# Hybrid encoder block, down-projection: the gating of the last two blocks of columns stands in the sixth product

## The chip, the cores and the metric

The kernel runs on one core of one Trainium2 chip. The metric is the device time of one execution in microseconds (us); several executions are timed and their median is given. Engines: PE multiplies matrices (TensorE), DVE, ACT and POOL work on vectors, SP issues the DMAs.

## What is computed

One layer of a streaming encoder on x of 2048 frames x 1024 columns in fp32. Only the end of the second sub-layer matters here:

```python
val, gte = jnp.split(u, 2, axis=-1)
x = x + (1 + gate2[:, None, :]) * ((val * jax.nn.silu(gte)) @ w_down[l])
return rms_norm(x, g_final)
```

The hidden matrix `val * silu(gte)` is 2048 x 2816, `w_down` is 2816 x 1024. `x` on the right is the residual after the first sub-layer, called x2 in the kernel.

## The kernel before

**Products.** The up- and the down-projection are multiplied by a scheme of Strassen's kind: each operand is cut into 2 x 2 blocks, and seven products of sums of blocks take the place of eight products. The down-projection (lines 1526 to 1683) runs the seven as a loop over p = 0 to 6; the text calls p = 5 the sixth product and p = 6 the seventh. A product is 1024 frames by 512 columns, summed over 1408 hidden columns, so 11 slices q of 128. The frames are eight tiles tt of 128. Each fp32 value is split into a high and a low part (`pinned_parts`, line 1405), and PE does three matmuls per slice and tile: high by high, high by low, low by high; 24 per slice, 264 per product.

**Order on PE.** The slices of a product go in groups, (0,1,2), (3,4), (5,6), (7), (8,9,10). Within a group PE takes the tiles in the order 0, 2, 3, 4, 1, 5, 6, 7, and for each the slices of the group (line 1675). A tile's result is read out of PSUM (`evict`) right behind its last slice in the last group. The results of tiles 0 and 1 lie in one PSUM tile `v`, the others have a tile `d` each.

**Loads and preparations.** `load_down` (1395) issues three DMAs from SP for a slice: two halves of the hidden columns (`hid_s`) into `ring`, a pool of 10 buffers, and the weight (`wd_s` or `w_down`) into a tile `h`. `prep_down` (1410) makes their parts: ACT copies the high parts (line 1406), POOL subtracts for the low part of the weight, DVE for the low parts of the two halves, `wua` (tiles 0 to 3) and `wub` (tiles 4 to 7) (line 1407). `next_down` (1423) prepares one slice. Ahead of a group of slices starting at g, slices up to g + 5 are prepared (PD = 6), so the sixth product's loop prepares its slices 3 to 10 and the seventh's 0 to 2.

**Order on the other engines.** `pin` keeps every instruction of this part in the order of the code on its engine. Work on results is spread among the preparations: `evict` puts generators into `todo`, and `do_later` (line 1637) takes a number of steps of them after each preparation (DL = 5, so the five steps of one tile). Steps of POOL that need a sum of squares from ACT follow one preparation later (`behind_y`).

**The end of the block.** After the sixth product, u holds what the blocks share, v the fourth product. The generator `c22` of a tile makes v = u + v, y = v x gt2 (the gate), y = y + x2 on POOL, u = u x gt2, x21 = x21 + u. `norm_y` lets ACT sum the squares of y and POOL multiply y by the gain. The seventh product is then added to x21, which gives the other half of the row; `finish` scales both by the root and stores them. `gt2` already holds the gate for both halves of the columns. `load_x2` (1556) loads the residual in four DMAs of 512 KB into the tiles h_5 (x22) and h_6 (x21); before, it is called for the last two blocks at the last group of the sixth product.

Of the kernel before, what the change touches and what calls it, by code (L numbers as in the profile page):

```python
# [8 lines left out]
F = mybir.dt.float32  # L9
# [3 lines left out]
ALU = mybir.AluOpType  # L13
# [3 lines left out]
P = 128  # L17
# [3 lines left out]
CH = 512  # L21
# [26 lines left out]
def hybrid_block(ctx, tc, x, c, w_ada, b_ada, g1, w_in, w_fg2, b_fg2, g_gla, w_out, g2,  # L48
                 w_up, w_conv, b_conv, w_down, g_fin, out):
    nc = tc.nc  # L50
    act, dve, pool, pe, dma = nc.scalar, nc.vector, nc.gpsimd, nc.tensor, nc.sync
# [8 lines left out]
    def sb(stack, name, bufs, side=None):  # L60
        return stack.enter_context(tc.tile_pool(name=name, bufs=bufs, side=side, reuse_waits="tile"))
# [1034 lines left out]
    sums = early_sums()  # L1096
    with in_order(("PE",)):
        for n in range(last_step):
# [16 lines left out]
            v = n - LEAD  # L1115
# [3 lines left out]
            if 0 <= v < N:  # L1119
                value(v)  # L1120
                u, s = divmod(v, 4)
# [34 lines left out]
    DL = 5  # L1156
# [284 lines left out]
    for n in range(2 * NF):  # L1441
        half, f = divmod(n, NF)
# [11 lines left out]
        if n == MW[0] - 2:  # L1454
            gt2 = eone.tile([P, D], F, name="gt2")
# [70 lines left out]
    with est as st:  # L1526
        yp = sb(st, "yp", 1)
        smalle = sb(st, "smalle", 4)
        gfin = yp.tile([P, D], F, name="gfin")
# [26 lines left out]
        def load_x2(i, blk, n):  # L1556
            tiles, ts = eight(i)
            for k, t_ in enumerate(ts):
                pin(dma.dma_start(out=t_, in_=x2_s[k // 2 * 2 + blk][k % 2 * 2 * P:(k % 2 + 1) * 2 * P, n * CH:(n + 1) * CH]
                                  .rearrange("(a p) n -> p a n", p=P)))  # L1560
            return tiles

        def tt_(eng, o, a, b, op):
            pin(eng.tensor_tensor(out=o, in0=a, in1=b, op=op))  # L1564

        nsl = [slice(n * CH, (n + 1) * CH) for n in range(2)]
        u, v = eight(3)[0], eight(4)[0]
        ys, sums, late, todo, behind_y = {}, {}, [], [], []

        def square(tt, y, tag):  # L1570

            ss = smalle.tile([P, 1], F, name=tag)
            junk = raw(None)
            pin(act.activation(out=junk, in_=y, func=AF.Square, scale=D ** -0.5, accum_out=ss))
            return ss

        def first_y(tt, n, x2):

            y = ys[tt]
            tt_(pool, y, y, x2, ALU.add)  # L1580

            def norm_y():
                sums[tt] = square(tt, y, f"ss{tt}")
                tt_(pool, y, y, gfin[:, nsl[n]], ALU.mult)
            behind_y.append(norm_y)
            yield

        def second_y(blk, n, tt, y):
            late.append(finish(blk, n, tt, y, square(tt, y, "ss"), ys[tt], sums[tt]))
            next(late[-1])  # L1590
            for g_ in late[-1 - LC:-LC]:
                next(g_)

        def mid():
            if late:
                next(late[-1])

        def evict(p, tt, ps):
            if p == 0:
                pin(act.activation(out=u[tt], in_=ps, func=AF.Copy))  # L1600
            elif p == 1:
                ys[tt] = yp.tile([P, CH], F, name=f"y{tt}")
                tt_(dve, ys[tt], ps, gt2[:, nsl[0]], ALU.mult)
                todo.append(first_y(tt, 0, x2[tt]))
            elif p == 2:
                tt_(dve, u[tt], ps, u[tt], ALU.add)
            elif p == 3:
                pin(act.activation(out=v[tt], in_=ps, func=AF.Copy))
            elif p == 4:
                y = raw(None)  # L1610
                tt_(dve, y, ps, u[tt], ALU.add)
                mid()
                tt_(dve, y, y, gt2[:, nsl[1]], ALU.mult)
                tt_(dve, y, y, x2[tt], ALU.add)
                second_y(0, 1, tt, y)
            elif p == 5:
                tt_(dve, u[tt], ps, u[tt], ALU.add)

                def c22(tt=tt, x22=x2[tt], x21=x2_last[tt]):
                    ys[tt] = yp.tile([P, CH], F, name=f"y{tt}")  # L1620
                    tt_(dve, v[tt], u[tt], v[tt], ALU.add)
                    yield
                    tt_(dve, ys[tt], v[tt], gt2[:, nsl[1]], ALU.mult)
                    yield
                    yield from first_y(tt, 1, x22)
                    tt_(dve, u[tt], u[tt], gt2[:, nsl[0]], ALU.mult)
                    yield
                    tt_(dve, x21, x21, u[tt], ALU.add)
                    yield
                todo.append(c22())  # L1630
            else:
                y = raw(None)
                tt_(dve, y, ps, x2_last[tt], ALU.add)
                mid()
                second_y(1, 0, tt, y)

        def do_later(n):

            for f_ in behind_y:
                f_()  # L1640
            behind_y.clear()
            for _ in range(n):
                while todo and next(todo[0], True):
                    todo.pop(0)

        acc = {}
        for p in range(7):
            begin = p not in (1, 4)
            for g in groups:
                while done < min(p * NQ2 + g[0] + PD, 7 * NQ2):  # L1650
                    next_down()
                    done += 1
                    if g[-1] != NQ2 - 1 or p < 6:
                        do_later(DL)
                last = g[-1] == NQ2 - 1
                if last and p in (4, 6):
                    do_later(len(todo) * 8)
                    do_later(0)
                if last and p in (1, 4, 5):
                    x2 = load_x2(5, p // 5, int(p != 1))  # L1660
                    if p == 5:
                        x2_last = load_x2(6, 1, 0)
                for tt in (0, 2, 3, 4, 1, 5, 6, 7):
                    if g[0] == 0 and begin:
                        if tt < 2:
                            t_ = pds[0].tile([P, HT], F, name="v") if tt == 0 else t_
                            acc[tt] = t_[:, tt * CH:(tt + 1) * CH]
                        else:
                            acc[tt] = pds[1].tile([P, CH], F, name=f"d{tt}")
                    ps = acc[tt]  # L1670
                    tsl = slice(tt % 4 * P, (tt % 4 + 1) * P)
                    for q in g:
                        hd, w = hids[p, q, tt // 4], w_d[p, q]
                        for m, (l_, r_) in enumerate(((0, 0), (0, 1), (1, 0))):
                            pin(pe.matmul(out=ps, lhsT=hd[:, l_, tsl], rhs=w[:, r_], start=begin and q == 0 and m == 0,  # L1675
                                          stop=q == NQ2 - 1 and m == 2, skip_group_check=not begin))
                    if last:
                        evict(p, tt, ps)
            if p in (4, 6):
                next(late[-1])  # L1680
                for g_ in late[-LC:]:
                    next(g_)
                late.clear()
# [25 lines left out]
```

## Time and profile before

| | |
|---|---|
| three executions | 2638.04, 2641.04, 2641.20 us |
| median | 2641.04 us |
| the profiled execution | 2639.18 us |
| its span, first to last instruction | 2637.5 us |
| PE busy | 2516.4 us, 95% |
| DVE, ACT, POOL busy | 1734.3, 1326.7, 1259.3 us |
| mean granted clock of PE | 0.988 of full |

The time of an execution holds 1.7 us around the span of its instructions. All times in the rows below count from the start of the span. Busy shares are of the whole program; the down-projection is the last 437 us of it. A timeline row gives the start, the duration, the engine, the line, the operation and its operands without buffer numbers (`x1` to `x27` is how many instructions the row merges), and, in brackets, how long the engine was idle before and what released it. POOL's rows for the end of the block have line 1564, that of the helper `tt_`; the tile names tell them apart: `h` tiles hold u, v, x2 and the parts of weights, `y` the first half of a row, `gt` the gate, and the residual's DRAM name reads `x_s`.

### The profile page before, as it was taken

To read this page: it belongs to the slowest core of one execution; us is meant where nothing else is said; L and a number is where in the kernel's file an instruction comes from. 1 tells how busy PE (TensorE), PEld (TensorE's weight loads), DVE (VectorE), ACT (ScalarE), POOL (GpSimd) and SP (SyncE) were. 2 spreads that over 40 slices of the span, in tenths; PEclk is the share of its full clock that TensorE was granted. 3 is DMA by queue.
4 is the path that set the end of the run, shared out by engine and by line. 5 is a ranking of instruction groups with operands and counts; after the bars stand their busy time and mean duration, and the time that the engine had idled before them with its cause. 6 is when DMAs were issued, how large, how long until landed. Compare 5 with 4: busy or idle time off the path is not lost. (4 is left out here: it accounts for less than half of the span.)

```text
span 2637.5 us, 36661 instructions
## 1 busy us (share of the span) xinstructions
PE 2516.4 (95%) x12118; PEld 2063.4 (78%) x12118; DVE 1734.3 (66%) x2332; ACT 1326.7 (50%) x2416; POOL 1259.3 (48%) x1074
## 2 busy tenths in 40 slices
PE   5899999999899999999989999989999999999998
PEld 5788778888678777777768888868888887888886
DVE  6525642144887999999668777776555556454668
ACT  4523234232776888888544444455455544333343
POOL 2202121121654656777346655677676663262336
PEclk9999999999999999999989999999999999999999
DMA  8657953576875544555555555576566557544472
GB/s 287 186 168 239 304 190 118 178 221 178 240 237 164 141 131 144 162 171 156 179 184 187 186 183 180 184 247 224 178 209 216 184 187 244 186 144 128 156 273 98
DMA packets 420558, 499.47 MB, mean 189 GB/s; under 512 B 38270, under 2 KB 262796, under 8 KB 418320
## 3 DMA queue, kind: packets, MB, share of 16 engines
q1 hardware_dynamic: 420368, 497.12, 59.1%
q8 instruction: 96, 1.57, 0.3%
q14 instruction: 94, 0.77, 0.1%
HBM read 330.81 MB, written 166.20 MB: 188 GB/s over the span
## 5 line engine op out<-in xcount | busy, mean ns | idle before, releaser
L1009 POOL TENSOR_TENSOR bt<-bt,om 128x512 f32<-128x512 f32 (+2 forms) x320 | 314.7, 988 | 219.5 <-DVE om L1007 121.5
L1186 POOL TENSOR_TENSOR wub<-ring,wub 128x512 fp32r<-128x512 f32 x172 | 239.5, 1404 | 180.7 <-ACT wub L1185 178.8
L1257 PE MATMUL v<-h,wub 128*128 128x512 f32 x1056 | 251.9, 395 | 14.1 <-DVE v L1261 14.1
L1257 PE MATMUL v<-h,wua 128*128 128x512 f32 x1056 | 259.6, 395 | 4.0 <-DVE eh L912 4.0
L1257 PE MATMUL g<-h,wub 128*128 128x512 f32 x1056 | 255.8, 391 | 2.9 <-DVE g L1261 2.9
L1007 DVE TENSOR_TENSOR_SCAN om<-sg,om,zero 128x513 f32<-128x513 f32 x189 | 240.5, 1273 | 16.0 <-ACT sg L1001 14.6
L1257 PEld LDWEIGHTS v<-h,wub 128*128 128x128 f32 x1056 | 200.7, 191 | 59.4 <-DVE v L1261 9.8
L1257 PEld LDWEIGHTS v<-h,wua 128*128 128x128 f32 x1056 | 199.8, 189 | 49.4 <-ACT wub L1185 4.2
L1257 PEld LDWEIGHTS g<-h,wub 128*128 128x128 f32 x1056 | 199.3, 189 | 45.4 <-DVE g L1261 3.3
L1186 POOL TENSOR_TENSOR wua<-ring,wua 128x512 fp32r<-128x512 f32 x129 | 179.4, 1399 | 115.9 <-ACT wua L1185 111.2
L1675 PE MATMUL d<-h,wub 128*128 128x512 f32 x924 | 222.9, 391 | 0.0
L1407 POOL TENSOR_TENSOR h<-h,h 128x512 fp32r<-128x512 f32 x77 | 114.0, 1483 | 213.1 <-ACT h L1406 190.0
L70 PE MATMUL tr<-ident,bt 128*128 128x128 f32 x1120 | 180.1, 277 | 35.6 <-DVE al L131 24.1
L131 DVE TENSOR_TENSOR al<-tr,ah 128x512 fp32r<-128x512 f32 (+1 forms) x320 | 193.0, 603 | 19.4 <-ACT ah L130 18.8
L1675 PEld LDWEIGHTS d<-h,wub 128*128 128x128 f32 x924 | 173.5, 188 | 37.6
L287 POOL TENSOR_TENSOR wr<-wst,wr 128x1024 fp32r<-128x1024 f32 x28 | 69.7, 2496 | 278.0 <-ACT wr L286 278.0
L130 ACT ACTIVATE ah<-tr 128x512 fp32r<-128x512 f32 (+1 forms) x320 | 179.7, 562 | 25.4 <-PE tr L70 25.1
L70 PEld LDWEIGHTS tr<-ident,bt 128*128 128x128 f32 x1120 | 126.7, 140 | 82.9 <-DVE al L131 34.8
L1334 DVE SCALAR_TENSOR_TENSOR cval<-v,conv_w,cval 128x1023 f32<-128x1023 f32 x44 | 56.4, 1282 | 182.5 <-ACT cval L1326 172.7
L1002 ACT ACTIVATE bt<-z 128x512 f32<-128x512 f32 (+2 forms) x320 | 173.7, 543 | 0.0
L401 PE MATMUL mm<-wr,hh 128*128 128x512 f32 (+1 forms) x448 | 169.7, 379 | 3.6 <-DVE vt L131 2.1
L403 PE MATMUL mm<-wr,hl 128*128 128x512 f32 (+1 forms) x448 | 167.8, 375 | 0.0
(312 smaller groups left out, 6010.2 us busy)
## 6 DMA issues: line engine op xcount, KB each, us to landing
ring<-in_w_up_dram SPq DMA_DIRECT2D x154, 256.0 KB, 3.8
ring<-hid_s SPq DMA_DIRECT2D x154, 256.0 KB, 4.2
wst<-in_w_in_dram SPq DMA_DIRECT2D x45, 512.0 KB, 7.6
wu_s<-ring SPq DMA_DIRECT2D x88, 256.0 KB, 2.4
hid_s<-cval SPq DMA_DIRECT2D x88, 256.0 KB, 2.3
ring<-wu_s SPq DMA_DIRECT2D x88, 256.0 KB, 4.7
kt<-k_hl SPq DMA_DIRECT2D x80, 256.0 KB, 3.3
vt<-v_hl SPq DMA_DIRECT2D x80, 256.0 KB, 3.2
```

Of the source, the lines that this page charges most:

```text
L70: pe.transpose(out=o, in_=i, identity=ident)
L130: act.activation(out=hi, in_=ps, func=AF.Copy)
L131: dve.tensor_tensor(out=lo, in0=ps, in1=f32(hi), op=ALU.subtract)
L401: pe.matmul(out=ps[:, :n], lhsT=hh[:, k, sl], rhs=wh, start=k == 0, stop=False)
L403: pe.matmul(out=ps[:, :n], lhsT=hl[:, k, sl], rhs=wh, start=False, stop=k == KD - 1)
L1002: act.activation(out=b1, in_=z[:, :w], func=AF.Sigmoid, scale=0.125)
L1007: dve.tensor_tensor_scan(out=om[:, 0:n_][:, ::-1], data0=beta[:, 0:n_][:, ::-1], data1=zero[0][:, 0:1].broadcast_to([P, n_]), initial=firs ...
L1009: pool.tensor_tensor(out=b1, in0=b1, in1=om[:, 1:w + 1], op=ALU.mult)
L1186: eng.tensor_tensor(out=t_[:, 1], in0=src, in1=f32(t_[:, 0]), op=ALU.subtract)
L1257: pe.matmul(out=ps, lhsT=lhsT, rhs=rhs, start=begin and k == 0 and m == 0, stop=k == KH - 1 and m == 2, skip_group_check=not begin)
L1407: pin(eng.tensor_tensor(out=t_[:, 1], in0=src, in1=f32(t_[:, 0]), op=ALU.subtract))
L1675: pin(pe.matmul(out=ps, lhsT=hd[:, l_, tsl], rhs=w[:, r_], start=begin and q == 0 and m == 0, stop=q == NQ2 - 1 and m == 2, skip_group_che ...
```

## The change

The work of `c22` is divided in two. A new generator `ahead_of_last` does what needs no sixth product: v = u + v, u = u x gt2, v = v x gt2, x21 = x21 + u, v = v + x22 (POOL). It is put into `todo` for all tiles at the start of the sixth product, so its steps stand among that product's preparations, and `load_x2` for the last two blocks is called at the start of the sixth product as well. The eviction of the sixth product writes the result twice, multiplied by each half of the gate, into y and u; `last_sums` then makes y = y + v on POOL and x21 = x21 + u on DVE, two steps per tile, among the seventh product's preparations.

```diff
--- before.py
+++ after.py
@@ -1614,25 +1614,39 @@
                 tt_(dve, y, y, x2[tt], ALU.add)
                 second_y(0, 1, tt, y)
             elif p == 5:
-                tt_(dve, u[tt], ps, u[tt], ALU.add)
-
-                def c22(tt=tt, x22=x2[tt], x21=x2_last[tt]):
-                    ys[tt] = yp.tile([P, CH], F, name=f"y{tt}")
-                    tt_(dve, v[tt], u[tt], v[tt], ALU.add)
-                    yield
-                    tt_(dve, ys[tt], v[tt], gt2[:, nsl[1]], ALU.mult)
-                    yield
-                    yield from first_y(tt, 1, x22)
-                    tt_(dve, u[tt], u[tt], gt2[:, nsl[0]], ALU.mult)
+                ys[tt] = yp.tile([P, CH], F, name=f"y{tt}")
+                tt_(dve, ys[tt], ps, gt2[:, nsl[1]], ALU.mult)
+                tt_(dve, u[tt], ps, gt2[:, nsl[0]], ALU.mult)
+
+                def last_sums(tt=tt, x21=x2_last[tt]):
+                    tt_(pool, ys[tt], ys[tt], v[tt], ALU.add)
+
+                    def norm_y():
+                        sums[tt] = square(tt, ys[tt], f"ss{tt}")
+                        tt_(pool, ys[tt], ys[tt], gfin[:, nsl[1]], ALU.mult)
+                    behind_y.append(norm_y)
                     yield
                     tt_(dve, x21, x21, u[tt], ALU.add)
                     yield
-                todo.append(c22())
+                todo.append(last_sums())
             else:
                 y = raw(None)
                 tt_(dve, y, ps, x2_last[tt], ALU.add)
                 mid()
                 second_y(1, 0, tt, y)
+
+        def ahead_of_last(tt, x22, x21):
+
+            tt_(dve, v[tt], u[tt], v[tt], ALU.add)
+            yield
+            tt_(dve, u[tt], u[tt], gt2[:, nsl[0]], ALU.mult)
+            yield
+            tt_(dve, v[tt], v[tt], gt2[:, nsl[1]], ALU.mult)
+            yield
+            tt_(dve, x21, x21, u[tt], ALU.add)
+            yield
+            tt_(pool, v[tt], v[tt], x22, ALU.add)
+            yield
 
         def do_later(n):
 
@@ -1646,20 +1660,21 @@
         acc = {}
         for p in range(7):
             begin = p not in (1, 4)
+            if p == 5:
+                x2, x2_last = load_x2(5, 1, 1), load_x2(6, 1, 0)
+                todo.extend(ahead_of_last(tt, x2[tt], x2_last[tt]) for tt in (0, 2, 3, 4, 1, 5, 6, 7))
             for g in groups:
                 while done < min(p * NQ2 + g[0] + PD, 7 * NQ2):
                     next_down()
                     done += 1
                     if g[-1] != NQ2 - 1 or p < 6:
-                        do_later(DL)
+                        do_later(DL if p < 6 else 2)
                 last = g[-1] == NQ2 - 1
-                if last and p in (4, 6):
+                if last and p in (4, 5, 6):
                     do_later(len(todo) * 8)
                     do_later(0)
-                if last and p in (1, 4, 5):
-                    x2 = load_x2(5, p // 5, int(p != 1))
-                    if p == 5:
-                        x2_last = load_x2(6, 1, 0)
+                if last and p in (1, 4):
+                    x2 = load_x2(5, 0, int(p != 1))
                 for tt in (0, 2, 3, 4, 1, 5, 6, 7):
                     if g[0] == 0 and begin:
                         if tt < 2:
```

DVE, the beginning of the sixth product. Before, the preparations of its slices 3, 4 and 5 follow each other (`wua`, `wub`: the two halves; `ring`: the loaded halves):

```order
L1407 TENSOR_TENSOR wua4_23734<-ring_23471,wua4_23734 128x512
L1407 TENSOR_TENSOR wub0_23737<-ring_23472,wub0_23737 128x512
L1407 TENSOR_TENSOR wua5_23749<-ring_23510,wua5_23749 128x512
L1407 TENSOR_TENSOR wub1_23752<-ring_23511,wub1_23752 128x512
L1407 TENSOR_TENSOR wua0_23764<-ring_23725,wua0_23764 128x512
L1407 TENSOR_TENSOR wub2_23767<-ring_23726,wub2_23767 128x512
```

and with the change (`h2_3` holds u, `h2_4` v, `h2_6` the residual x21, `gt2` the gate):

```order
L1407 TENSOR_TENSOR wua4_23750<-ring_23471,wua4_23750 128x512
L1407 TENSOR_TENSOR wub0_23753<-ring_23472,wub0_23753 128x512
L1564 TENSOR_TENSOR h2_4_0_21339<-h2_3_0_21335,h2_4_0_21339 128x512
L1564 TENSOR_TENSOR h2_3_0_21335<-h2_3_0_21335,gt2_16878 128x512
L1564 TENSOR_TENSOR h2_4_0_21339<-h2_4_0_21339,gt2_16878 128x512
L1564 TENSOR_TENSOR h2_6_0_23733<-h2_6_0_23733,h2_3_0_21335 128x512
L1407 TENSOR_TENSOR wua5_23770<-ring_23510,wua5_23770 128x512
L1407 TENSOR_TENSOR wub1_23773<-ring_23511,wub1_23773 128x512
L1564 TENSOR_TENSOR h2_4_1_21340<-h2_3_1_21336,h2_4_1_21340 128x512
```

Four operations of one tile stand behind each preparation, eight times in all.

DVE, the passage from the sixth to the seventh product. Before, each tile is evicted by one operation (`d7` is the last one's result), and between two preparations stand four operations of one tile:

```order
L1564 TENSOR_TENSOR h2_3_3_21338<-d6_23829,h2_3_3_21338 128x512
L1564 TENSOR_TENSOR h2_3_3_21338<-d7_23839,h2_3_3_21338 128x512
L1407 TENSOR_TENSOR wua3_24194<-ring_24035,wua3_24194 128x512
L1407 TENSOR_TENSOR wub5_24197<-ring_24036,wub5_24197 128x512
L1564 TENSOR_TENSOR h2_4_0_21339<-h2_3_0_21335,h2_4_0_21339 128x512
L1564 TENSOR_TENSOR y0_24200<-h2_4_0_21339,gt2_16878 128x512
L1564 TENSOR_TENSOR h2_3_0_21335<-h2_3_0_21335,gt2_16878 128x512
L1564 TENSOR_TENSOR h2_6_0_24097<-h2_6_0_24097,h2_3_0_21335 128x512
L1407 TENSOR_TENSOR wua4_24215<-ring_24074,wua4_24215 128x512
L1407 TENSOR_TENSOR wub0_24218<-ring_24075,wub0_24218 128x512
```

With the change each tile is evicted by two, and one operation stands between two preparations:

```order
L1564 TENSOR_TENSOR h2_3_2_21337<-d5_23850,gt2_16878 128x512
L1564 TENSOR_TENSOR y6_24226<-d6_23860,gt2_16878 128x512
L1564 TENSOR_TENSOR h2_3_3_21338<-d6_23860,gt2_16878 128x512
L1564 TENSOR_TENSOR y7_24238<-d7_23870,gt2_16878 128x512
L1564 TENSOR_TENSOR h2_3_3_21338<-d7_23870,gt2_16878 128x512
L1407 TENSOR_TENSOR wua3_24250<-ring_24091,wua3_24250 128x512
L1407 TENSOR_TENSOR wub5_24253<-ring_24092,wub5_24253 128x512
L1564 TENSOR_TENSOR h2_6_0_23733<-h2_6_0_23733,h2_3_0_21335 128x512
L1407 TENSOR_TENSOR wua4_24267<-ring_24130,wua4_24267 128x512
L1407 TENSOR_TENSOR wub0_24270<-ring_24131,wub0_24270 128x512
L1564 TENSOR_TENSOR h2_6_1_23734<-h2_6_1_23734,h2_3_1_21336 128x512
```

SP. Before, the eight loads of the residual (`x2_s`) stand behind the loads of the seventh product's slice 4 (`h2_0_2_24078`):

```order
L1399 DMA ring_24075<-hid_s1_2_121 128x512
L1402 DMA h2_0_2_24078<-wd_s3_129 128x512
L1559 DMA h2_5_0_24089<-x2_s1_101 128x2x512
L1559 DMA h2_5_1_24090<-x2_s1_101 128x2x512
L1559 DMA h2_5_2_24091<-x2_s3_103 128x2x512
L1559 DMA h2_5_3_24092<-x2_s3_103 128x2x512
L1559 DMA h2_6_0_24097<-x2_s1_101 128x2x512
L1559 DMA h2_6_1_24098<-x2_s1_101 128x2x512
L1559 DMA h2_6_2_24099<-x2_s3_103 128x2x512
L1559 DMA h2_6_3_24100<-x2_s3_103 128x2x512
L1399 DMA ring_24185<-hid_s0_2_114 128x512
L1399 DMA ring_24186<-hid_s1_2_121 128x512
```

With the change they stand right behind the last store of the fifth product's results, ahead of the loads of the sixth product's slice 5 (`h2_0_0_23745`):

```order
L1548 DMA out_0_dram<-ring_23698 128x512
L1559 DMA h2_5_0_23725<-x2_s1_101 128x2x512
L1559 DMA h2_5_1_23726<-x2_s1_101 128x2x512
L1559 DMA h2_5_2_23727<-x2_s3_103 128x2x512
L1559 DMA h2_5_3_23728<-x2_s3_103 128x2x512
L1559 DMA h2_6_0_23733<-x2_s1_101 128x2x512
L1559 DMA h2_6_1_23734<-x2_s1_101 128x2x512
L1559 DMA h2_6_2_23735<-x2_s3_103 128x2x512
L1559 DMA h2_6_3_23736<-x2_s3_103 128x2x512
L1399 DMA ring_23741<-hid_s0_5_117 128x512
L1399 DMA ring_23742<-hid_s1_5_124 128x512
L1402 DMA h2_0_0_23745<-wd_s2_128 128x512
```

Eleven slices' loads are passed. On POOL, `ahead_of_last` puts one sum behind each of the first eight preparations of the sixth product; its operations in the seventh stay three per tile. On PE and ACT the order stays.

## Rows read from the trace of the kernel before

**Rows 1.** Page, part 1: busy us (share of the span) and instructions.
```profile
PE 2516.4 (95%) x12118; PEld 2063.4 (78%) x12118; DVE 1734.3 (66%) x2332; ACT 1326.7 (50%) x2416; POOL 1259.3 (48%) x1074
```

**Rows 2.** Chain of waits, end of the program: start us, us, what.
```profile
2609.99 1.69 POOL h L1407
...
2613.05 7.07 PE d L1675 x27
```

**Rows 3.** Timeline, PE: start us, us, engine, line, operation, output<-inputs, count, [idle time before <-what ended it].
```profile
2502.47 2.20 PE L1675 MATMUL v<-h,wua 128*128 128x512 f32 x9
...
2518.87 1.52 PE L1675 MATMUL v<-h,wua 128*128 128x512 f32 x6
...
2546.20 2.20 PE L1675 MATMUL v<-h,wua 128*128 128x512 f32 x9
...
2562.60 2.20 PE L1675 MATMUL v<-h,wua 128*128 128x512 f32 x9
...
2606.34 1.75 PE L1675 MATMUL v<-h,wua 128*128 128x512 f32 x7
...
2611.71 1.34 PE L1675 MATMUL v<-h,wua 128*128 128x512 f32 x2 [3.63 <-POOL h L1407]
...
2621.99 6.34 PE L1675 MATMUL d<-h,wub 128*128 128x512 f32 x27
```

**Rows 4.** Windows: busy us of PE, PEld, DVE, ACT, POOL (instructions), clock, DMA share, GB/s.
```profile
2612.00:2614.00 2.00, 2.00 (x5) 1.46 (x6) 2.00 (x3) 0.00 (x0) 1.34 (x1) 0.50 0.00 0
2614.00:2616.00 2.00, 2.00 (x8) 1.59 (x8) 1.93 (x4) 0.00 (x0) 0.71 (x1) 0.78 0.00 0
```

**Rows 5.** Timeline, DVE, seventh product, a turn of one frame tile.
```profile
2565.33 0.69 DVE L1564 TENSOR_TENSOR y<-h,gt 128x512 f32<-128x512 f32 x1
...
2566.66 1.67 DVE L1564 TENSOR_TENSOR h<-h,h 128x512 f32<-128x512 f32 x1
...
2568.25 1.79 DVE L1407 TENSOR_TENSOR wua<-ring,wua 128x512 fp32r<-128x512 f32 x1
...
2572.38 0.69 DVE L1564 TENSOR_TENSOR y<-h,gt 128x512 f32<-128x512 f32 x1
```

**Rows 6.** Timeline, POOL, the same turn.
```profile
2566.10 1.68 POOL L1564 TENSOR_TENSOR y<-y,h 128x512 f32<-128x512 f32 x1 [17.18 <-DVE y L1564]
2567.74 1.75 POOL L1407 TENSOR_TENSOR h<-h,h 128x512 fp32r<-128x512 f32 x1
```

**Rows 7.** Windows, sixth product, where the loads run; columns as in rows 4.
```profile
2528.00:2531.00 3.00, 3.00 (x15) 2.48 (x14) 3.00 (x4) 2.03 (x5) 1.83 (x2) 1.00 1.05 388
```

**Rows 8.** Timeline, SP: the loads of slice 6.5 and the x2 loads.
```profile
2513.41 1.32 SPq L1399 DMA_DIRECT2D ring<-hid_s  x2
...
2514.85 0.44 SPq L1402 DMA_DIRECT2D h<-wd_s  x1
...
2535.41 5.83 SPq L1559 DMA_DIRECT2D h<-x_s  x8
```

**Rows 9.** Timeline, ACT: first copy of slice 6.5.
```profile
2518.36 0.63 ACT L1406 ACTIVATE h<-h 128x512 fp32r<-128x512 f32 x1 [3.53 <-DMA h<-wd_s]
```

**Rows 10.** Instructions on the tile x_s, 2534 to 2542: landing of the x2 loads.
```profile
DMA to landing us min/median/max: 6.7/9.1/11.4
```

**Rows 11.** Timeline, DVE, sixth product: subtractions, and the first eviction.
```profile
2512.78 1.37 DVE L1407 TENSOR_TENSOR wua<-ring,wua 128x512 fp32r<-128x512 f32 x1 [1.05 <-ACT wua L1406]
...
2520.84 0.68 DVE L1407 TENSOR_TENSOR wub<-ring,wub 128x512 fp32r<-128x512 f32 x1
...
2548.44 0.69 DVE L1564 TENSOR_TENSOR h<-v,h 128x512 f32<-128x512 f32 x1 [0.68 <-PE v L1675]
```

**Rows 12.** Line 131 (duration ns min/median/max); the page, part 5.
```profile
L131 DVE TENSOR_TENSOR al<-tr,ah x320: 387/662/692, 672.0 to 1289.2; 128x512 fp32r<-128x512 f32 x128, 128x256 fp32r<-128x256 f32 x32
...
L1009 POOL TENSOR_TENSOR bt<-bt,om 128x512 f32<-128x512 f32 (+2 forms) x320 | 314.7, 988 | 219.5 <-DVE om L1007 121.5
```

## Prediction

> **Names.** The seven products of the down-projection are counted from one, the eleven slices of each from zero: slice 6.4 is slice 4 of the sixth product (index 5 in the code). The *preparation* of a slice is three copies on ACT, one subtraction on POOL (weight) and two on DVE (the two halves of the hidden columns, first wua, then wub). A slice is 24 matmuls for the eight frame tiles.
>
> **What bounds the kernel now.** I read the page first: PE is busy for 95% of the span [rows 1], so time can only come from stretches where PE waits. The chain of waits shows one in the part that the change touches: just before the end it leaves PE and runs through POOL's subtraction for a weight [rows 2]. The PE timeline gives its price. The sixth product runs from 2502.47 to 2562.60, which is 60.13 us or 0.228 us for each of 264 matmuls. The seventh would end at 2562.60 + 60.13 = 2622.73, and ends at 2621.99 + 6.34 = 2628.33: 5.60 us are lost [rows 3]. Of these 3.63 are the idle time before slice 7.10's low weight part; the other 1.97 pass right behind it, where the granted clock is 0.50 and then 0.78, between the 1.2 and 2.4 GHz levels [rows 4].
>
> Why is that weight late? In the seventh product DVE needs 7.05 us for one tile's turn (2565.33 to 2572.38) [rows 5], against 24 x 0.228 = 5.47 us that PE spends on a slice. The turn holds six DVE and three POOL operations, and their rows show that they go one at a time: POOL's sum ends at 2567.78, and DVE's addition, begun at 2566.66, ends at 2568.33, 0.55 later; POOL's next ends 1.16 after that, DVE's next 0.55 later again [rows 5, 6]. So a turn is six times about 0.6 plus three times about 1.15.
>
> **The change, by counts.** Per frame tile, four DVE operations leave the seventh product and one comes back; four DVE and one new POOL operation go into the sixth product's preparations; the sixth eviction has two DVE operations in place of one. In all 16 DVE and 8 POOL operations are added. The eight x2 loads move on SP from behind the load of slice 7.4 to before that of slice 6.5.
>
> *What goes.* With three DVE and three POOL operations, a turn of the seventh product takes 3 x 0.6 + 3 x 1.15 = 5.25 us, under PE's 5.47. The 5.60 us can go: **-5.6**.
>
> *The loads.* Eight x2 tiles of 0.524 MB stand in front of a stretch of SP's loads in which the queue moved 388 GB/s at a DMA share of 1.05 [rows 7]: 1.35 us a tile, 10.8 us for all. Before, slice 6.5's three loads (0.786 MB, 2.03 us at that rate) went out from 2513.41 [rows 8] and ACT could start on them at 2518.36 [rows 9], 4.95 us later, so 2.9 us come on top of the transfer. The first tile that DVE adds to is the fifth load: 5 x 1.35 + 2.9 = 9.65 us, so 2523.1. The loads of before took 6.7 to 11.4 us to land [rows 10]; that spread, 2520 to 2525, bounds it. The trace's rate can be weighed against a rule: the Trainium skill (Perfetto Trace Analysis, Roofline) says that a core working alone can draw about 435 GB/s from its 16 DMA engines. The trace shows 388 where the engines are full. By the page's figure the eight tiles would take an estimated 9.6 us, and the sum below would be 1.2 us smaller.
>
> *DVE behind them.* DVE works in order. Tile 0's fourth operation (the addition to x2) waits until 2523.1, and behind it stands the preparation of slice 6.4, which before was done at once behind 6.3's (first of these at 2512.78 [rows 11]). Now its first half ends at 2523.1 + 2 x 0.65 = 2524.4. PE wants it for the sixth matmul of the group that starts at 2518.87 [rows 3], at 2520.0. PE idles **4.4 us**, and if this costs clock as the idle time of 3.63 did, 2 more. POOL's new sum waits less long, for the first x2 tile.
>
> *DVE as the bound.* Slice 6.5 lands 10.8 later, at 2529.2. Its last DVE operation ended 3.16 us behind its landing before (2520.84 + 0.68 [rows 11], less 2518.36): 2532.3. From there each preparation carries one tile's four operations: six DVE and two POOL operations, the turn of rows 5 without one POOL operation, 7.05 - 1.15 = 5.9 us. No row shows this mix. It lies between 4.1 (six at 0.69, nothing held up) and 7.05; I take 5.9 because the rows nearest to it have the same operations in the same turn. It is more than PE's 5.47, so DVE never catches up. Slice 6.10 is five turns on, at 2561.8, its first half 0.6 before: 2561.2. PE wants it seven matmuls into the last group, 2546.20 + 1.6 = 2547.8 [rows 3]. That is 13.4 us late, more than the 6.4 that PE has lost by itself, so 13.4 holds and the first wait is inside it. The rest of the product, 16.4 - 1.6 = 14.8 us, brings PE to 2576.0, or 2578 at a lower clock.
>
> *The evictions.* DVE's sixth turn ends at 2567.7. Two bare preparations (7.1, 7.2; two DVE and one POOL operation, 2.4 us each) come next: 2572.5. Only then do the evictions run. Before they cost nothing, one 0.69 us operation per tile at PE's pace [rows 11]. Now the seventh product's first matmul needs the bank pair of tiles 0 and 1 free, and tile 1 is the fifth evicted: ten operations of 0.65, 2579.0. Their inputs come from PSUM; an operation of that kind never took over 0.692 us in 320 instances, in a stage that had POOL at work on 314.7 us of sums [rows 12], so I count no hold-up. PE is ready before that, so the seventh product starts at 2579.0, not 2562.60: **+16.4**.
>
> **Sum:** 16.4 - 5.6 = **+10.8 us**. The profiled execution took 2639.18 us, so 2650.0. The median of the runs before is 2641.04, 1.9 above it; the prediction is for a median: **2651.8**. The stretch behind the last matmul (9.2 us to the end of the span) stays. ACT's copies stay as many, and in their order.
>
> **Rivals.**
> *Only the first wait (12%).* If DVE's and POOL's operations hold each other up less in this mix, a turn stays under 5.47, DVE catches up within the sixth product, and the change trades one wait for another: 4.4 + 2.0 - 5.6 = +0.8, 2641.8. For it: in the same stretch of before, some DVE subtractions took 0.68 [rows 11]. Against: those are the ones with no POOL operation under way.
>
> *Faster (6%).* The new POOL and DVE work fits into the sixth product, where both have idle time now. This needs the fifth x2 tile by about 2518.7, so that slice 6.4 is ready at 2520.0, and a turn under 5.47. Then only the gain is left: -5.6, 2635.4. Against it: a landing under 5.3 us, where the shortest seen is 6.7 [rows 10], and eight tiles need 10.8 in all.
>
> *The seventh product falls behind as well (12%).* Slice 7.10 is due 2606.34 - 2562.60 + 1.6 = 45.3 us after the product's start [rows 3], at 2624.3. DVE ends its 16 evictions at 2572.5 + 16 x 0.65 = 2582.9 and has eight turns to go: at 5.25 us, 2624.9. That is on the edge; a head start of POOL during the evictions decides for me. With 6.0 a turn it would be 2630.9: 6.6 late and 2 for the clock, +19.4, 2660.4.
>
> That the change doesn't do what it says is excluded by the order of instructions, where the work stands in the sixth product on DVE, POOL and SP.
>
> **Numbers.** My forecast has 70%. A measurement of this kernel can tell about 0.2%, 5.3 us, from no change. The forecast and the third rival are slower by more: 82%. The first rival is the same: 12%. The second is faster, just past the bound: 6%. Range: with a turn of 7.05, six turns add 6.9, with 2 for the clock +19.7, 2660.7, which also takes in the third rival; I end at 2661. Downwards the forecast with a turn of 5.5 is 2.4 less, with the x2 tiles 1.5 early 3.9 less; half way from there to the first rival is about 2643, where I stop. Left out are the faster case and most of the first rival.
>
> **What the profile would show.** Right: DVE idle until about 2523 for an x2 load; PE idle 4 us near 2520 for wua; a second, longer gap near 2556 in the sixth product's last group; evictions from about 2572, as a row without gaps; the seventh product's first matmul near 2579, with PE waiting for DVE; no gap after it, last matmul near 2639. Wrong: evictions that begin near 2548 at PE's pace (first rival), no gap at 2520 (second), a gap behind 2615 (third). Turns of DVE in the sixth product of less than 5.5 us would break the step on which most rests.

## The result, and the profile after

The changed kernel takes **2658.94 us** (median of 4 runs, 2650.61 to 2661.38) against 2640.14 for the kernel before (4 runs, 2638.04 to 2641.2). The ratio is 1.0069, with a 95% interval of 1.0057 to 1.0082: slower by 18.8 us, where the prediction had 10.8 and a range up to 2661.

Every number below is from the profiled execution of each kernel. The changed kernel's has a span of 2659.6 us and a time of 2661.38, the longest of its four. Page, part 1: busy us (share of the span) and instructions.

```profile
PE 2526.8 (95%) x12118; PEld 2069.1 (78%) x12118; DVE 1749.5 (66%) x2348; ACT 1327.6 (50%) x2416; POOL 1271.0 (48%) x1082
```

Beside [rows 1] this shows the 16 added DVE and 8 added POOL operations and the same 12118 matmuls. PE is busy 10.4 us longer with them, though it has no more to do: some ran at a lower clock. The PE timeline shows where (start us, us, engine, line, operation, output<-inputs, count, [idle time before <-what ended it]).

```profile
2505.15 2.20 PE L1690 MATMUL v<-h,wua 128*128 128x512 f32 x9
...
2524.03 0.50 PE L1690 MATMUL v<-h,wua 128*128 128x512 f32 x1 [1.41 <-POOL h L1407]
2528.97 0.79 PE L1690 MATMUL v<-h,wua 128*128 128x512 f32 x1 [4.44 <-DVE wua L1407]
...
2559.98 0.96 PE L1690 MATMUL v<-h,wua 128*128 128x512 f32 x3 [1.07 <-POOL h L1407]
2565.86 1.22 PE L1690 MATMUL v<-h,wua 128*128 128x512 f32 x2 [4.92 <-POOL h L1407]
...
2579.18 4.21 PE L1690 MATMUL v<-h,wua 128*128 128x512 f32 x9 [3.87 <-DVE h L1564]
...
2590.20 2.21 PE L1690 MATMUL v<-h,wua 128*128 128x512 f32 x9
...
2644.16 6.34 PE L1690 MATMUL d<-h,wub 128*128 128x512 f32 x27
```

The sixth product runs from 2505.15 to 2590.20: 85.05 us where it took 60.13 [rows 3]. PE stops in three places, for slice 6.4, for slice 6.10 (with a short wait for 6.9 ahead of it), and in the last group. The idle times are 1.41 + 4.44 + 1.07 + 4.92 + 3.87 = 15.71 us. Of the other 9.2 us of the 24.9 lost, 7.8 are matmuls behind the stops that take longer than 0.228 us each: 2.3 us in the 13 from 2528.97 to 2534.25, 2.7 in the 20 from 2565.86 to 2573.07, and 2.8 in the 36 from 2579.18 to 2590.20. Most of the rest is the last matmul ahead of each stop, which runs to its end (the lone one at 2524.03 takes 0.50 us). The windows show the granted clock behind the stops (columns as in rows 4):

```profile
2529.00:2532.00 3.00, 3.00 (x7) 2.42 (x8) 2.96 (x5) 0.00 (x0) 0.48 (x1) 0.50 1.05 399
...
2566.00:2568.00 2.00, 2.00 (x5) 1.61 (x6) 1.97 (x4) 0.00 (x0) 0.00 (x0) 0.50 0.57 176
...
2580.00:2582.00 2.00, 2.00 (x6) 1.52 (x6) 2.00 (x4) 0.63 (x1) 0.00 (x0) 0.50 0.08 23
```

PE is busy all through each of these windows, but the clock is 0.50, the 1.2 GHz level, behind each of the three long stops. It had idled 3.9 to 4.9 us just before.

The seventh product lasts from 2590.20 to 2644.16 + 6.34 = 2650.50, which is 60.3 us: the 5.60 us of [rows 3] are gone, and no matmul in it waits. The tail is 9.1 us, as before. In sum the spans differ by 22.1 us: 24.9 - 5.6 + 0.1 of small differences, and 2.68 by which the sixth product started later than in [rows 3], upstream of all that was changed. In four more kernels with the same code up to there (experiments 1, 3, 4 and 7 below) that start lay between 2497.26 and 2505.77. It is scatter, and the medians, 18.8 apart, leave most of it out.

DVE's timeline shows the fourth operation of tile 0, the starts of three turns, and the end of the product:

```profile
2527.62 0.69 DVE L1564 TENSOR_TENSOR h<-h,h 128x512 f32<-128x512 f32 x1 [8.26 <-DMA h<-x_s]
...
2551.09 1.78 DVE L1407 TENSOR_TENSOR wua<-ring,wua 128x512 fp32r<-128x512 f32 x1
...
2557.02 1.79 DVE L1407 TENSOR_TENSOR wua<-ring,wua 128x512 fp32r<-128x512 f32 x1
...
2562.93 1.76 DVE L1407 TENSOR_TENSOR wua<-ring,wua 128x512 fp32r<-128x512 f32 x1
...
2568.81 1.77 DVE L1407 TENSOR_TENSOR wua<-ring,wua 128x512 fp32r<-128x512 f32 x1
...
2572.18 1.77 DVE L1407 TENSOR_TENSOR wua<-ring,wua 128x512 fp32r<-128x512 f32 x1
...
2577.85 0.68 DVE L1564 TENSOR_TENSOR y<-v,gt 128x512 f32<-128x512 f32 x1
2578.45 0.68 DVE L1564 TENSOR_TENSOR h<-v,gt 128x512 f32<-128x512 f32 x1
```

DVE idles 8.26 us for an x2 tile, and then its turns are 5.93 and 5.91 us long (2551.09, 2557.02, 2562.93; the last of these begins slice 6.10). From 2568.81 it makes three bare preparations in 9.04 us, the last two of them from 2572.18. Tile 0's two evictions follow, and as the second ends (2578.45 + 0.68 = 2579.13), the matmuls that idled 3.87 us start, at 2579.18. Those are tile 1's, still in the sixth product. POOL's timeline of the same stretch:

```profile
2564.10 1.70 POOL L1407 TENSOR_TENSOR h<-h,h 128x512 fp32r<-128x512 f32 x1
...
2568.36 1.66 POOL L1564 TENSOR_TENSOR h<-h,h 128x512 f32<-128x512 f32 x1 [2.56 <-DVE h L1564]
2569.98 6.79 POOL L1407 TENSOR_TENSOR h<-h,h 128x512 fp32r<-128x512 f32 x4
```

The weight of slice 6.10 ends at 2564.10 + 1.70 = 2565.80, and PE's matmul starts at 2565.86. Each sum of POOL waits for DVE (2.56 us), and the weights queue behind it. Four of them run only from 2569.98, in the same stretch as DVE's bare preparations.

ACT's first copy of slice 6.5, which [rows 9] has at 2518.36, comes here behind the x2 loads:

```profile
2533.59 0.63 ACT L1406 ACTIVATE h<-h 128x512 fp32r<-128x512 f32 x1 [16.08 <-DMA h<-wd_s]
```

### The profile page after: what moved, and what is told of

It is laid out like the page before. It is cut to its first block, busy times and chain, and to the rows that moved or that the text cites. A ratio compares the mean times of both kernels' runs of the same rounds, so it can differ in the third digit from the quotient of the medians.

```text
span 2659.6 us, 36691 instructions
## 1 busy us (share of the span) xinstructions
PE 2526.8 (95%) x12118; PEld 2069.1 (78%) x12118; DVE 1749.5 (66%) x2348; ACT 1327.6 (50%) x2416; POOL 1271.0 (48%) x1082
## 5 line engine op out<-in xcount | busy, mean ns | idle before, releaser
L1257 PEld LDWEIGHTS g<-h,wub 128*128 128x128 f32 x1056 | 199.3, 189 | 45.3 <-DVE g L1261 3.3
L131 DVE TENSOR_TENSOR al<-tr,ah 128x512 fp32r<-128x512 f32 (+1 forms) x320 | 192.9, 603 | 19.4 <-ACT ah L130 18.8
```

The costliest lines, as they stand in the source:

```text
L131: dve.tensor_tensor(out=lo, in0=ps, in1=f32(hi), op=ALU.subtract)
L1257: pe.matmul(out=ps, lhsT=lhsT, rhs=rhs, start=begin and k == 0 and m == 0, stop=k == KH - 1 and m == 2, skip_group_check=not begin)
```

## Experiments

**Theory.** The change's loss is a chain in the sixth product: the x2 loads come too late for tile 0 and delay slice 6.5; the added operations then make DVE's turn longer than the time PE gives it; and the late evictions hold PE once more through the PSUM tile that tiles 0 and 1 share. Rivals: the loads alone are the loss; or it lies in the work added to DVE, so that one more operation there makes it worse. Timed beside the experiments, the kernel before took 2639.99 us (23 runs, first to fourth) and 2639.85 (22 runs, fifth to seventh).

| kernel | median us (runs) | ratio to before, 95% |
|---|---|---|
| 1 loads alone | 2640.27 (10) | 0.9999, 0.9990 to 1.0008 |
| 2 half of the loads a product earlier | 2651.26 (6) | 1.0046, 1.0031 to 1.0062 |
| 3 tile 0 evicted behind tile 1's matmuls | 2653.18 (6) | 1.0049, 1.0033 to 1.0066 |
| 4 before, two operations less | 2634.13 (10) | 0.9979, 0.9968 to 0.9989 |
| 5 shorter turn, loads apart | 2643.75 (12) | 1.0017, 1.0007 to 1.0027 |
| 6 one DVE operation moved to the evictions | 2633.08 (12) | 0.9978, 0.9967 to 0.9988 |
| 7 the new sum on DVE, not POOL | 2652.44 (6) | 1.0055, 1.0040 to 1.0071 |

The change itself has 1.0057 to 1.0082. The intervals of 2, 3 and 7 reach into it, so by the times alone their gains of 6 to 8 us over the change are not clear of scatter; what these three show is read from their traces.

**1. The loads alone.** The changed kernel without the operations that it had moved ahead.

```diff
         def ahead_of_last(tt, x22, x21):
-            tt_(dve, v[tt], u[tt], v[tt], ALU.add)
-            yield
...
-            tt_(pool, v[tt], v[tt], x22, ALU.add)
             yield
```

> Changed kernel without the work ahead: the four DVE and one POOL operation per tile of the new generator are left out (the output lacks the fourth product's share and the first part of the residual), the x2 loads stay in front of slice 6.5, the double evictions and the short turn of the seventh product stay. My theory (the loads cost little by themselves, DVE's pace behind them costs): slice 6.5 still lands near 2531 on the clock of before, so PE stops 3 to 4 us near 2530 and loses about 2 to the clock, the seventh product loses nothing: about before, 2637 to 2643. Rival (the x2 loads in front of the slices cause most of the +18.8): 2652 to 2658.

Measured 2640.27: no difference from before. Timeline of PE (the seventh product is the last row):

```profile
2501.72 2.20 PE L1681 MATMUL v<-h,wua 128*128 128x512 f32 x9
...
2532.42 2.82 PE L1681 MATMUL v<-h,wua 128*128 128x512 f32 x4 [3.21 <-ACT wua L1406]
2535.54 1.34 PE L1681 MATMUL v<-h,wua 128*128 128x512 f32 x2 [0.30 <-POOL h L1407]
...
2569.33 2.20 PE L1681 MATMUL v<-h,wua 128*128 128x512 f32 x9
```

The sixth product takes 67.6 us, 7.5 more than before: 3.51 idle, of which ACT's copy of slice 6.5 ends 3.21 and its weight on POOL 0.30, and 4.0 beside it, nearly all at a lower clock (0.50 from 2534 to 2538). That pays back what the seventh product gains, and no more: the eight loads in front of slice 6.5 cost a stop by themselves, but all of the 18.8 us by which the change is slower needs the added operations, and with them DVE's wait for the x2 tile.

**2. Half of the loads a product earlier.** The tiles that DVE adds go out at the start of the fifth product.

```diff
+            if p == 4:
+                x2_last = load_x2(6, 1, 0)
             if p == 5:
-                x2, x2_last = load_x2(5, 1, 1), load_x2(6, 1, 0)
+                x2 = load_x2(5, 1, 1)
```

> Changed kernel with four of the eight x2 loads (those for x21) issued at the start of the fifth product. My theory (two separate costs: DVE waits for the fifth load, then its turns of 5.9 us are longer than PE's 5.47): the stop of 4.4 us near 2520 for wua goes, slice 6.5 lands 5.4 earlier, but slice 6.10 is still about 8 us late and the evictions still late: 2649 to 2654. Rival A (the wait for the load is the whole loss): 2640 to 2643. Rival B (only the amount of work on DVE counts): as the change, 2656 to 2661.

Measured 2651.26, 7.7 less than the change. Timeline of PE:

```profile
2501.83 2.20 PE L1692 MATMUL v<-h,wua 128*128 128x512 f32 x9
...
2521.41 1.22 PE L1692 MATMUL v<-h,wua 128*128 128x512 f32 x2 [2.12 <-POOL h L1407]
...
2556.84 1.22 PE L1692 MATMUL v<-h,wua 128*128 128x512 f32 x2 [4.91 <-POOL h L1407]
...
2570.17 4.21 PE L1692 MATMUL v<-h,wua 128*128 128x512 f32 x9 [3.86 <-DVE h L1564]
```

and of DVE, slice 6.5:

```profile
2525.75 1.36 DVE L1407 TENSOR_TENSOR wua<-ring,wua 128x512 fp32r<-128x512 f32 x1 [3.24 <-ACT wua L1406]
```

The stop for wua is gone, and 2.12 us for a weight are left of the first one. Yet the other two stops stand as they were (4.91 and 3.86). Slice 6.10 comes 55.0 us after the product's start, 9.7 past the 45.3 at which PE wants it. The loads have a part in this too: four of them still stand ahead of slice 6.5, and DVE waits 3.24 us for it. Without that wait slice 6.10 would come an estimated 9.7 - 3.2 = 6.5 us late, which is what the turn makes.

**3. Tile 0 evicted behind tile 1's matmuls.** In the sixth product's last group alone.

```diff
-                    if last:
+                    if last and p == 5:
+                        if tt == 1:
+                            evict(p, 0, acc[0])
+                        if tt != 0:
+                            evict(p, tt, ps)
+                    elif last:
```

> Changed kernel with the sixth product's eviction of tile 0 written behind tile 1's matmuls, so that tile 1's matmuls, which write the same PSUM tile, have no late reader ahead of them. My theory (the third stop, 3.87 us before tile 1's last slices, is a wait for tile 0's eviction, and the low clock behind it costs 2 to 3 more): the seventh product starts 5 to 6 us earlier, 2652 to 2654. Rival (the evictions must be over before the seventh product starts in any case, so the wait only moves to there): 2658 to 2661, with a gap at the start of the seventh product.

Measured 2653.18, 5.8 less than the change. Timeline of PE:

```profile
2565.84 1.22 PE L1690 MATMUL v<-h,wua 128*128 128x512 f32 x2 [4.91 <-POOL h L1407]
...
2575.03 2.20 PE L1690 MATMUL v<-h,wua 128*128 128x512 f32 x9
...
2584.07 2.32 PE L1690 MATMUL v<-h,wua 128*128 128x512 f32 x9 [0.66 <-DVE h L1564]
```

Tile 1's matmuls (2575.03) no longer wait, and the seventh product, whose first matmul needs both tiles evicted, waits 0.66. From slice 6.10 to its start PE takes 18.2 us, against 24.3 in the change. That pins the third stop on the shared PSUM tile, of which tiles 0 and 1 have one half each: the wait is between operations on the same tile, though they touch different columns of it.

**4. The gain alone.** The kernel before, without two of the operations of its seventh turn and with nothing added to the sixth product.

```diff
                     yield from first_y(tt, 1, x22)
-                    tt_(dve, u[tt], u[tt], gt2[:, nsl[0]], ALU.mult)
-                    yield
-                    tt_(dve, x21, x21, u[tt], ALU.add)
                     yield
```

> Kernel before with two of the four DVE operations per tile of the seventh product's turn left out (the gating of u and its addition to x21; the output lacks them). My theory (a turn of 7.05 us makes the stop of 3.63 and its clock loss; with 5.85 slice 7.10 is ready about 4 us in time): 5.6 us less than before, 2633 to 2636, no gap in the last group. Rival (the stop has another cause, as the landing of the last loads): 2638 to 2641.

Measured 2634.13, 5.9 less than before: the prediction's -5.6, by itself. Timeline of PE, start and end of the seventh product:

```profile
2558.47 2.20 PE L1672 MATMUL v<-h,wua 128*128 128x512 f32 x9
...
2612.43 6.34 PE L1672 MATMUL d<-h,wub 128*128 128x512 f32 x27
```

It takes 60.30 us, as in the change.

**5. The idea of the change with a shorter turn.** The sum of u and v moves into the fourth product's evictions, half of the loads go out in the fifth product, the other half only ahead of the second group of slices of the sixth, and POOL's sums follow one per preparation. Three DVE operations per tile are left in the turn.

```diff
             elif p == 3:
-                pin(act.activation(out=v[tt], in_=ps, func=AF.Copy))
+                tt_(dve, v[tt], ps, u[tt], ALU.add)
...
-            tt_(pool, v[tt], v[tt], x22, ALU.add)
+            tt_(dve, v[tt], v[tt], gt2[:, nsl[1]], ALU.mult)
...
+            if p == 4:
+                x2_last = load_x2(6, 1, 0)
...
+                if p == 5 and g[0] == 3:
+                    x2 = load_x2(5, 1, 1)
+                    join = [0, 2, 3, 4, 1, 5, 6, 7]
...
+                    if p == 5 and join:
+                        j_ = join.pop(0)
+                        tt_(pool, v[j_], v[j_], x2[j_], ALU.add)
```

> The change's idea with its three stops taken away: the sum u + v is made by the eviction of the fourth product (DVE from PSUM in place of ACT's copy), the x21 loads go out at the start of the fifth product, the x22 loads and POOL's sums behind the first three preparations of the sixth. A turn in the sixth product has five DVE and two POOL operations, or mostly five and one. My theory (exclusive turns of about 0.6 per DVE and 1.15 per POOL operation, 5.3 us or less, under PE's 5.47): no gap in the sixth or seventh product, 5 to 6 us under before: 2633 to 2636. Rival (work moved into the sixth product slows it whatever its order, as DMA and POOL are busier there): 2640 to 2650.

Measured 2643.75: a miss. It is 15.2 us faster than the change, but still slower than before. The profiled execution, at 2650.1, is the longest of the twelve. Timelines of PE and of DVE:

```profile
2506.29 2.20 PE L1694 MATMUL v<-h,wua 128*128 128x512 f32 x9
...
2556.08 0.50 PE L1694 MATMUL v<-h,wua 128*128 128x512 f32 x1 [4.08 <-DVE wua L1407]
...
2567.79 4.21 PE L1694 MATMUL v<-h,wua 128*128 128x512 f32 x9 [3.45 <-DVE h L1564]
```

```profile
2516.60 1.37 DVE L1407 TENSOR_TENSOR wua<-ring,wua 128x512 fp32r<-128x512 f32 x1 [1.05 <-ACT wua L1406]
...
2550.04 0.68 DVE L1407 TENSOR_TENSOR wua<-ring,wua 128x512 fp32r<-128x512 f32 x1
...
2555.34 0.68 DVE L1407 TENSOR_TENSOR wua<-ring,wua 128x512 fp32r<-128x512 f32 x1
```

The turn is 5.3 us, under PE's 5.47, as expected, and the load stop is gone. But 5.47 was the wrong measure. The preparations of slices 6.3 to 6.10 begin 10.3 us into the product (2516.60), and the first half of slice 6.10 is wanted 45.6 us into it, for the ninth matmul of the last group. Between lie seven turns and that half itself (0.7 us): 34.6 us for seven, or **4.9 us a turn**. Here the seven took 38.7 us (2516.60 to 2555.34), slice 6.10 came 4.2 us late, and the stop at the shared PSUM tile came with it. So a turn of three added operations per tile and one sum on POOL, 5.3 us, doesn't fit into the sixth product even where no load is late.

**6. One operation moved to the evictions.** The kernel before, where the sum of u and v is made from PSUM, in the evictions of the fourth and the sixth product; the seventh product's turn has one DVE operation less, and each eviction of the sixth has two in place of one.

```diff
             elif p == 3:
-                pin(act.activation(out=v[tt], in_=ps, func=AF.Copy))
+                tt_(dve, v[tt], ps, u[tt], ALU.add)
...
             elif p == 5:
+                tt_(dve, v[tt], ps, v[tt], ALU.add)
                 tt_(dve, u[tt], ps, u[tt], ALU.add)
...
-                    tt_(dve, v[tt], u[tt], v[tt], ALU.add)
-                    yield
...
-                        do_later(DL)
+                        do_later(DL if p < 6 else 4)
```

> Kernel before with only the sum u + v moved: into the evictions of the fourth product (v = product + u) and of the sixth (two evictions, u and v, both from PSUM). The seventh product's turn has five DVE and three POOL operations. My theory: 7.05 - 0.6 = 6.4 us a turn, slice 7.10's weight 4.5 us earlier, just in time: 2634 to 2637, with at most a gap under 1 us in the last group. Rival (evictions that take twice as long hold PE up at the end of the sixth product): 2639 to 2643.

Measured **2633.08**, a little under what was expected: it beats both kernels, by 6.8 and 25.9 us. Timelines of PE, DVE and POOL:

```profile
2502.55 2.20 PE L1674 MATMUL v<-h,wua 128*128 128x512 f32 x9
...
2562.68 2.20 PE L1674 MATMUL v<-h,wua 128*128 128x512 f32 x9
...
2616.64 6.34 PE L1674 MATMUL d<-h,wub 128*128 128x512 f32 x27
```

```profile
2548.52 1.29 DVE L1564 TENSOR_TENSOR h<-v,h 128x512 f32<-128x512 f32 x2 [0.68 <-PE v L1674]
...
2568.19 1.78 DVE L1407 TENSOR_TENSOR wua<-ring,wua 128x512 fp32r<-128x512 f32 x1
...
2574.52 1.78 DVE L1407 TENSOR_TENSOR wua<-ring,wua 128x512 fp32r<-128x512 f32 x1
```

```profile
2605.57 1.74 POOL L1407 TENSOR_TENSOR h<-h,h 128x512 fp32r<-128x512 f32 x1
```

Both products take 60.1 to 60.3 us, without a gap. The two evictions of a tile take 1.29 us and still wait 0.68 for PE, so the second costs PE nothing. The seventh turn is 6.33 us instead of 7.05 [rows 5]; slice 7.10's weight is ready at 2607.31. PE wanted it 45.3 us into the product, at 2608.0: 0.7 us to spare.

**7. The new sum on DVE.** The changed kernel, in which DVE makes the sum that the change gave to POOL: one more operation for the engine that binds, one less for POOL.

```diff
-            tt_(pool, v[tt], v[tt], x22, ALU.add)
+            tt_(dve, v[tt], v[tt], x22, ALU.add)
```

> Changed kernel with POOL's sum v + x22 of the new generator done by DVE: one more operation on DVE, which is late, and one less on POOL. My theory (operations of DVE and POOL on SBUF go one at a time, so a turn is 0.6 per DVE and 1.15 per POOL operation): a turn in the sixth product falls from 5.9 to about 5.4 us, slice 6.10 is ready 2 to 3 us earlier, 2654 to 2657. Rival (DVE's own operations set the turn): turn 6.5 us, slice 6.10 3 us later, 2661 to 2665.

Measured 2652.44, 6.5 less than the change and under what was expected; the profiled execution, at 2648.75, is the shortest of the six. Timelines of PE and DVE:

```profile
2497.26 2.20 PE L1690 MATMUL v<-h,wua 128*128 128x512 f32 x9
...
2559.63 0.80 PE L1690 MATMUL v<-h,wua 128*128 128x512 f32 x1 [4.35 <-DVE wua L1407]
...
2569.26 2.33 PE L1690 MATMUL v<-h,wua 128*128 128x512 f32 x9 [0.55 <-DVE h L1564]
...
2577.61 2.20 PE L1690 MATMUL v<-h,wua 128*128 128x512 f32 x9
```

```profile
2542.58 0.68 DVE L1407 TENSOR_TENSOR wua<-ring,wua 128x512 fp32r<-128x512 f32 x1
...
2548.03 0.68 DVE L1407 TENSOR_TENSOR wua<-ring,wua 128x512 fp32r<-128x512 f32 x1
...
2564.31 0.68 DVE L1407 TENSOR_TENSOR wua<-ring,wua 128x512 fp32r<-128x512 f32 x1
...
2567.92 0.68 DVE L1564 TENSOR_TENSOR y<-v,gt 128x512 f32<-128x512 f32 x1
```

The turn falls from 5.93 to 5.45 us although DVE has seven operations in it instead of six. That refutes the rival which counts DVE's operations alone. But the shorter turn did not bring slice 6.10 earlier, as was expected of it: PE takes it up 62.4 us after the product's start (2559.63 less 2497.26), against 60.7 in the change. The x2 tiles came later in this execution (DVE idles 7.99 us for them, until 23.3 us into the product instead of 22.5), and DVE's turn behind slice 6.5 took 9.4 us, while POOL made one weight after another. The gain lies behind slice 6.10, from where PE needs 18.0 us to the seventh product's start (2577.61), against 24.3 in the change: POOL's weights no longer queue behind a sum that waits for DVE, and are done early. DVE's three bare preparations then take 3.61 us (2564.31 to 2567.92) instead of 9.04, tile 0 is evicted sooner, and the third stop is 0.55 instead of 3.87.

## Why the prediction was right, and where its size was off

The sign, the mechanism and the order of events came as forecast. Times as us after the sixth product's start take the 2.68 of scatter out:

| step | predicted | measured |
|---|---|---|
| x2 tile lets tile 0's fourth operation go | 20.6 | 22.5 |
| ACT starts slice 6.5 | 26.7 | 28.4 |
| DVE's turn | 5.9 | 5.93 |
| slice 6.10's first half, on DVE, ready | 58.7 | 59.5 |
| PE goes on with slice 6.10 | 58.7 | 60.7 |
| evictions start | 70.0 | 72.7 |
| seventh product starts | 76.5 | 85.05 |
| seventh product lasts | 60.1 | 60.3 |
| last matmul's end to the end | 9.2 | 9.1 |

The prediction had PE wait for the first half of slice 6.10 on DVE. PE waited 1.2 us longer, for the slice's weight on POOL, which stands behind a sum that waits for DVE.

**-5.6 for the seventh product: right.** It is seen in the change, and by itself in experiment 4 (-5.9).

**The loads: right in kind, 1.8 us short.** The first load was issued at 2516.10 and the fifth tile served DVE at 2527.62, 11.5 us later, where the sum had 9.65. In the windows from 2516 to 2522 the queue moved 314 GB/s, and from then on 324 to 392, while the sum had 388 throughout. By the 435 GB/s of the page that the prediction weighed (the Trainium skill, Perfetto Trace Analysis, Roofline) the tiles would have landed earlier than the sum had it; they landed later. The page gives the figure as a bound of the 16 engines, and the trace agrees with a bound: its rates lie under it. The stop it makes for wua is there, 4.44 us as against 4.4, with 1.41 for a weight ahead of it that had not been named.

**The turn of 5.9: right, to 0.03.** The step on which most rested was to put in place of an unknown mix the nearest turn less one POOL operation. The reason for it held as well: a turn took 7.05 us with six DVE and three POOL operations, 6.33 with five and three, 5.93 with six and two, 5.45 with seven and one, 5.30 with five and two. A POOL operation adds about 1.1 and a DVE one 0.6 to 0.7, as they follow one another. The Trainium skill (SBUF — State Buffer, Who interferes with whom) states the rule behind this: a DVE instruction with two SBUF inputs contends with a GpSimd instruction that reads SBUF, and the pair of ports that they share is an exclusive lock. The traces agree: a DVE subtraction takes 0.68 us with no POOL operation under way, and 1.74 to 1.80 in the turns of the change, where POOL has one under way as it begins; the evictions, with one input in PSUM, stayed at 0.67 to 0.69, as in [rows 12].

**The +16.4: the step that failed, in its size.** It measured +24.9. The prediction had the evictions start at 70.0 and the seventh product's first matmul behind ten of them, 6.5 us on. The 8.5 us between 76.5 and 85.05 are three pieces:
- *The evictions start 2.7 later.* Of this 1.7 came with the loads (slice 6.5 at 28.4 instead of 26.7). Some 0.9 are the last two bare preparations, 2572.18 to 2577.85: 5.67 us instead of 2 x 2.4, since four weights on POOL run through them.
- *The wait stands at another place: 3.0.* The prediction named the bank pair of tiles 0 and 1, but only for the seventh product's first matmul. Tile 1's matmuls in the sixth product's last group write to the same PSUM tile, and wait for tile 0's eviction too. So PE goes on after two evictions (1.3 us), but then has 36 matmuls left, 8.2 us at full speed: 9.5 where ten evictions had 6.5. For the same reason the evictions are no row without gaps: after the first eight, DVE waits for PE. Experiment 3 shows that this is the cause: with that one order changed, 0.66 of wait is left, and PE needs 18.2 us from slice 6.10 to the seventh product instead of 24.3.
- *The clock: 2.8.* Those 36 matmuls took 11.0 us instead of 8.2 (2579.18 to 2590.20), the first of them at the clock of 0.50 that the windows show behind the third stop. The prediction counted the clock at nothing in the sum, since it let PE wait at the product's end. That held for the slow matmuls of 2566 to 2573, which the third stop hid: tile 1's had to wait until 2579.13 anyway. It didn't hold for those behind that stop.

That 2658.94 still lies in the range is in part luck. The upper end of 2661 was made for a turn of 7.05 us or for the third rival, and neither came.

**Rivals.** That only the first wait is left fell: even with half of the loads a product earlier (experiment 2) the other stops remain. Its point of decision, a turn under 5.47, was too lenient, as experiment 5 showed: DVE starts the preparations 10.3 us into the product and needs 4.9. The faster case fell with its first condition: the fifth x2 tile served DVE after 11.5 us, where it needed one under 5.3. That the seventh product falls behind as well did not happen. In the kernels tried, that product lost nothing at turns up to 6.33.

**What stays open.** The low clock could not be taken away by itself, so its 7.8 us are read from rows and not shown by a run. A kernel with both experiments 2 and 3 was not run, nor the change with all eight loads out of slice 6.5's way, so how the loss divides between the loads and the turn is estimated.

## What to carry to other kernels

Before moving work into a stage with idle time, count the time from the moment its engine is free there to the due time of the last thing that it must deliver, and divide by the turns in between (experiment 5: 34.6 us for seven); the pace of the consumer alone is too lenient. Where DVE and POOL both work on SBUF, add their times instead of taking the longer, as all the turns here did, and look for operations that can take an input from PSUM: moving one addition into evictions gave all of the gain (experiment 6). When an eviction may come late, look up which other tile shares its PSUM tile, and whose matmuls come next there.

## What the runs showed of the hardware that was not expected

A stop of PE costs more than its idle time: 15.71 us of idle time in the change came with 7.8 us lost in slower matmuls behind the stops, where the granted clock was 0.50 at first, and the 3.51 of experiment 1 with nearly 4. Moving an operation from POOL to DVE, the busier engine, made the contended turn shorter (5.93 to 5.45 us), and freed POOL's queue to run ahead: three preparations then took 3.61 us instead of 9.04.
